# Power tables of a state-space layer made once for all groups, and dealt out at pace 0.85

## The chip, the cores and the metric

One core of a Trainium2 chip. The metric is the device time of one execution in microseconds (us). Two times are compared: the kernel before and the kernel after the change, with the same inputs and outputs.

## What is computed

A backbone of two layers on 512 latent tokens and 256 context tokens of width 1024. Layer 0 is attention, layer 1 a bidirectional diagonal state-space layer (S5); each layer has a SwiGLU feed-forward part before and after its mixer, with RMS norms and modulation around every part. The S5 mixer has 64 groups of 16 channels, each with 64 complex states in each of two directions:

```python
dt = exp(log_step); a = exp(lam_re * dt) * (cos(lam_im * dt) + 1j * sin(lam_im * dt))
f  = (a - 1) / lam ;  bb = f * b
x[t] = a * x[t-1] + bb @ u[t] ;  y[t] = real(c @ x[t]) + d * u[t]     # forward and backward
```

The kernel does the recurrence in blocks of 8 tokens. For that it needs, for each group and state, the powers a^0 to a^8, and for 96 blocks the phases of u^k, where u is the unit part of a^8. They depend on the weights alone and can be made long before the layer.

## The kernel before

**Feed-forward parts.** Nearly all time goes to matmuls of 128x128 weight tiles with 512 latent and 256 context columns. To keep precision each f32 weight tile is split into a high part (`whi`, ScalarE, L760) and a low part (`wlo`, mostly VectorE, L770), and each product is three matmuls (`mm3`, L869 to L871). A part runs in four chunks of 6, 5, 5 and 6 hidden tiles. In a chunk each hidden tile has two `w13` rows (8 k steps each), then VectorE multiplies gate and up (`w13_out`, L1067), ScalarE writes the high part `gh` (L918) and VectorE the low part `gl` (L921); the `w2` rows of the chunk follow and need all its hidden tiles, the last one last.

**Crossings.** From one part to the next a planned order (`cross`, L2608) runs the last rows, the norm sums (POOL among others), the new norm and the first rows of the next part. While it runs, background work is held (`hush`).

**Background work.** `s5_task` (L1948) is a Python generator that makes the S5 tables. It is put on the list `bg` in the crossing from attention to the second feed-forward part, and `rate` is set to `S5RATE` there (L2668). When the program is written, every stretch of PE work calls `tick` (L813) with its charged time (columns / 2400 per matmul); unless held, `pump` (L700) adds charge x `rate` to a credit of at most 8.0 and runs the generator to its next `yield` as long as the credit is above 0. The number a yield gives is taken off the credit. So pace and yields decide where the instructions stand in each engine's queue; each engine works its queue in order. Whatever is left when `need("s5")` is called in the crossing to the S5 layer (L2676) is issued there in one piece.

**The tables.** An opening (L1966 to L2058, all on VectorE but two sines) makes a (`A1`), the factor `F` and the unit phases (`un`) for all 64 groups; its yields sum to 28.2. Then `table(m)` (L2071) runs eight times, for 8 groups each:
- `bb` from `s5bc` and `F` (L2078 to L2084, VectorE);
- `pm`, the powers 0 to 8, by three complex products (`pmul`, `cmul`), and `ua`, the phase and its six squarings (`sq`), of tiles with 8 groups (L2087 to L2107, VectorE); `cmul` is six instructions (L1954 to L1959);
- `s5pw`, the powers in two orders, by eight copies (L2111 to L2114, VectorE);
- four times for two groups each: `s5v` by six products (L2133 to L2135), copies into `s5Bd` (L2137 to L2141), all VectorE; six POOL instructions (L2175 to L2179); `wout`, transposes on PE (L2186); `kout`, eight small matmuls on PE (L2148) that need `s5v` and `s5Bd`; `kcopy` (L2155 to L2164);
- the phase table `s5T` by doublings on POOL from `ua` (L2206 to L2225).

The results go to DRAM by 20 stores a table on SP's queue (L2121), and the S5 layer loads them per 8 groups (L2267 to L2281). The yields of a table sum to 92.3: 1.5 for `bb`, 0.6 + 3 x 1.0 + 6 x 1.0 for `pm` and `ua`, 1.2 for `s5pw`, 49.9 for the four quarters, 3.5, and 26.6 for the phase table. In a quarter, 1.5 follow the `s5Bd` copies, 4.5 the POOL instructions, 1.5 more, then comes `kout`. Between the crossings' ends the two feed-forward parts charge 419.8 and 435.2 us of PE time.

Of the kernel before, what the change touches and what calls it, by code (L numbers as in the profile page):

```python
# [10 lines left out]
F32 = mybir.dt.float32  # L11
# [5 lines left out]
P = 128  # L17
# [10 lines left out]


SC = (-1.5, -1.5, -1.3, -0.8, -0.25)  # L30
S5RATE = 1.0
PAIR = 1
LPS = (2,)
CP = [3.0, 3.0, 1.0, 1.3]
# [377 lines left out]
class Model:  # L412
# [837 lines left out]
    def attn(self, a, parts):  # L1250
# [153 lines left out]
        def split_nodes(n, hi, lo, deps, prio, acq=(), alloc=None, pool=False):  # L1404

            def fh():
                if alloc:
                    alloc()
                o, i = hi()
                nc.scalar.activation(o, i, AF.Copy)  # L1410

            def fl():
                o, i = lo()
                (nc.gpsimd if pool else nc.vector).tensor_tensor(o, i, hi()[0].bitcast(F32), op=ALU.subtract)
            h = G.add(ACT, cost[ACT](n), fh, deps, prio, acq)
            l = G.add(POOL if pool else DVE, cost[POOL if pool else DVE](n), fl, [h], prio)
            return h, l
# [49 lines left out]
        def spread(box):  # L1467
            box["h"], box["l"] = [st["A"].tile([P, 512], F32R, tag="pt" + x, name=f"pt{x}{self.uid()}", bufs=4)
                                  for x in ("h", "l")]

        def turned(blocks, deps, prio):

            box = {}
            n = len(blocks) * P

            def ft():
                box["t"] = self.sbank()
                for i, (b, c) in enumerate(blocks):
                    nc.tensor.transpose(box["t"][:, i * P:(i + 1) * P], b["p"][:, c:c + P], self.ident)
            T = G.add(PE, 0.11 * len(blocks), ft, deps, prio, ("st",))  # L1480
            h, l = split_nodes(n, lambda: (box["h"][:, :n], box["t"][:, :n]), lambda: (box["l"][:, :n], box["t"][:, :n]),
                               [T], prio, ("pt",), alloc=lambda: spread(box))
            T.free["st"].append(l)
            return box, n, T, h, l

# [21 lines left out]
        def weighted(hd, keys, vt, deps):  # L1507
# [4 lines left out]
            for j, (kt, blocks, cols, dn) in enumerate(keys):  # L1512
                prio = hd + (j + 0.5) / 7
                tb, n, T, h, l = turned(blocks, dn, prio)
                reads.append(T)

# [431 lines left out]
    def s5_task(self):  # L1948
        nc, io = self.nc, self.io
        v = nc.vector  # L1950

        def cmul(eng, outr, outi, ar, ai, br, bi, t):

            eng.tensor_tensor(t[0], ar, br, op=ALU.mult)  # L1954
            eng.tensor_tensor(t[1], ai, bi, op=ALU.mult)
            eng.tensor_tensor(outr, t[0], t[1], op=ALU.subtract)
            eng.tensor_tensor(t[0], ar, bi, op=ALU.mult)
            eng.tensor_tensor(t[1], ai, br, op=ALU.mult)
            eng.tensor_tensor(outi, t[0], t[1], op=ALU.add)  # L1959

        def gen():
            self.s5_open()
            sb, pp = self.sb, self.pp
            G = 64
            new = lambda name, shape, dt=F32, pool=sb: pool.tile(shape, dt, name=name)
            dsk = new("s5d", [16, G])  # L1966
            nc.sync.dma_start(out=dsk, in_=io["s5d"])
            A1 = new("s5A1", [P, 2, G])
            un = new("s5un", [P, 2, G])
# [4 lines left out]
            for tag, k in (("s5t0", 4), ("s5t1", 4), ("s5t3", 1)):  # L1974
                w = sb.tile([P, k, G], F32, tag=tag, name="s5w_" + tag)
# [30 lines left out]
            n, r = t[0], t[1]  # L2006
# [40 lines left out]
            sq = lambda o, i, q: cmul(v, o[0], o[1], i[0], i[1], i[0], i[1], q)  # L2047
# [8 lines left out]
            v.tensor_copy(un[:, 0], u2[0])  # L2056
            v.tensor_copy(un[:, 1], u2[1])
            yield 2.0  # L2058
            NG = 2
            Bd = new("s5Bd", [P, 2, NG, 64])  # L2060
            nc.gpsimd.memset(Bd, 0.0)
# [9 lines left out]
            def table(m):  # L2071
                gs = slice(m * 8, m * 8 + 8)
# [10 lines left out]
                v.tensor_tensor(bb[:, 1], q[:, 0], q[:, 1], op=ALU.add)  # L2083
                v.tensor_scalar(ci, ci, -1.0, None, op0=ALU.mult)  # L2084
                yield 1.5

                pm = sb.tile([P, 2, 9, 8], F32, tag="s5pm", name=f"s5pm{m}")  # L2087
                ua = sb.tile([P, 2, 7, 8], F32, tag="s5ua", name=f"s5ua{m}")
                sc = sb.tile([P, 2, 4, 8], F32, tag="s5sc", name=f"s5sc{m}")
                v.memset(pm[:, 0, 0], 1.0)  # L2090
                v.memset(pm[:, 1, 0], 0.0)
                for c in (0, 1):
                    v.tensor_copy(pm[:, c, 1], A1[:, c, gs])
                    v.tensor_copy(ua[:, c, 0], un[:, c, gs])

                def pmul(lo, n):
                    s_, o_ = slice(1, n + 1), slice(lo + 1, lo + n + 1)
                    b0, b1 = (pm[:, c, lo:lo + 1].to_broadcast([P, n, 8]) for c in (0, 1))
                    cmul(v, pm[:, 0, o_], pm[:, 1, o_], pm[:, 0, s_], pm[:, 1, s_], b0, b1,
                         [sc[:, 0, 0:n], sc[:, 1, 0:n]])  # L2100
                yield 0.6
                for lo, n in ((1, 1), (2, 2), (4, 4)):
                    pmul(lo, n)
                    yield 1.0
                for k in range(6):
                    sq((ua[:, 0, k + 1], ua[:, 1, k + 1]), (ua[:, 0, k], ua[:, 1, k]), [sc[:, 0, 0], sc[:, 1, 0]])
                    yield 1.0  # L2107
                pw = sb.tile([P, 2, 2, 8, 8], F32, tag="s5pw", name=f"s5pw{m}")
                ge = lambda x: x.rearrange("p e g -> p g e")
                for c in (0, 1):  # L2110
                    v.tensor_copy(pw[0:64, 0, c], ge(pm[0:64, c, 7::-1]))  # L2111
                    v.tensor_copy(pw[64:128, 0, c], ge(pm[64:128, c, 0:8]))
                    v.tensor_copy(pw[0:64, 1, c], ge(pm[0:64, c, 8:0:-1]))
                    v.tensor_copy(pw[64:128, 1, c], ge(pm[64:128, c, 1:9]))  # L2114
                yield 1.2
                cost = 0.75
                later, stores = [], []

                def flush():
                    for o, x in stores:  # L2120
                        nc.sync.dma_start(out=o, in_=x)  # L2121
                    stores.clear()
                for hf in range(8 // NG):
                    hs = slice(hf * NG, hf * NG + NG)
                    S4 = [P, NG, 8, 16]

                    vk = [sb.tile([P, NG, 144], F32, tag=f"s5v{i}", name=f"s5v{m}{hf}{i}") for i in range(2)]
                    t2 = sb.tile(S4, F32, tag="s5v2", name=f"s5v2{m}{hf}")
# [14 lines left out]
                    def kout(vk=vk):  # L2143
                        ps = self.bank()
                        for g in range(NG):
                            o = ps[0:64, g * 144:(g + 1) * 144]
# [59 lines left out]
                n, ng = 96, 4  # L2206
                for g0 in range(0, 8, ng):
                    gg = slice(g0, g0 + ng)
                    T = [sb.tile([P, ng, n], F32, tag=f"s5t{i}", name=f"s5T{m}{g0}{i}") for i in (0, 1)]
                    R = [sb.tile([P, ng, 32], F32, tag=f"s5t{i}", name=f"s5R{m}{g0}{i}") for i in (2, 3)]  # L2210
                    g_.memset(T[0][:, :, 0:1], 1.0)
                    g_.memset(T[1][:, :, 0:1], 0.0)
                    k, lev = 1, 0
                    while k < n:
                        w = min(k, n - k)
                        ur, ui = (ua[:, c, lev, gg].unsqueeze(2).to_broadcast([P, ng, w]) for c in (0, 1))
                        cmul(g_, T[0][:, :, k:k + w], T[1][:, :, k:k + w], T[0][:, :, 0:w], T[1][:, :, 0:w], ur, ui,
                             [R[0][:, :, 0:w], R[1][:, :, 0:w]])
                        yield 0.8 + 0.015 * w * ng
                        flush()  # L2220
                        k, lev = k + w, lev + 1
                    for c in (0, 1):
                        stores.append((self.dr[m, :, c, gg], T[c]))
                    yield 2.0
                    flush()  # L2225
            for m in range(8):
                yield from table(m)
            self.bg_done.add("s5")
            yield 0.0
        return ("s5", gen())  # L2230


# [401 lines left out]
    def build(self):  # L2634
# [20 lines left out]
        def end_mods():  # L2655
# [12 lines left out]
        self.cross(attn, (0, 1), ffn01, (0, 2), a2, lambda: (self.yc.release(), self.bg.append(self.s5_task()),  # L2668
                                                           setattr(self, "rate", S5RATE)),
                   lambda: (attn.close(), self.ffn_pool()))  # L2670
# [223 lines left out]
```

## Time and profile before

| | us |
|---|---|
| three runs | 3020.44, 3026.11, 3029.89 (median 3026.11) |
| the profiled execution, its own time | 3023.44 |
| span of its profile | 3021.4 |
| mean granted TensorE clock | 0.97 |

The span is what the profiler saw from the first to the last instruction. Engines are PE (matmul), PEld (weight load beside it), DVE (VectorE), ACT (ScalarE), POOL (GpSimd) and SP (which issues transfers). Matmuls are pipelined: the length of one in a row of the timeline is longer than the distance to the next. A wait is put down to the work that released it last.

### The profile page before, as it was taken

Reading aid. Unit: us, or ns where it says so; the run is one execution under the profiler, and the core shown is the slowest. Engines: PE = TensorE matmul, PEld = TensorE weight load, DVE = VectorE, ACT = ScalarE, POOL = GpSimd, SP = SyncE. Lnnn points to the kernel's source line nnn. Section 1 sums busy time; section 2 is a strip of 40 time slices with the busy share of each in tenths; the row PEclk is TensorE's granted clock in tenths of the full one; section 3 lists DMA queues with packets and bytes.
Section 4 is the critical chain, followed back from the end, with each engine's and each line's share of the span. In section 5 each row is a group of like instructions: output and inputs, shape, how many; then the busy total and the mean of one; then the engine's idle time right before and its main releaser. Section 6 shows DMA issues by size and latency. Waiting matters only on the chain. (4 is left out here: it accounts for less than half of the span.)

```text
span 3021.4 us, 42503 instructions
## 1 busy us (share of the span) xinstructions
PE 2839.2 (94%) x16008; PEld 2453.4 (81%) x16008; DVE 1921.5 (64%) x3621; ACT 1084.0 (36%) x1897; POOL 902.7 (30%) x1281
## 2 busy tenths in 40 slices
PE   4999989989999989999999899999998899999997
PEld 3888778878778778888887788888887897988886
DVE  8798989675588577465465765456337695543344
ACT  3432232344587652222222432222124444432222
POOL 4122222252354351334434534434405100300001
PEclk9999999999799999999999999999999899999998
DMA  6365556633000222323232333232323463232332
GB/s 245 105 217 185 193 183 231 220 108 120 5 24 22 92 97 86 101 70 95 87 99 82 104 110 89 87 99 71 99 67 104 174 214 98 93 109 92 100 101 70
DMA packets 140813, 343.59 MB, mean 114 GB/s; under 512 B 13632, under 2 KB 61248, under 8 KB 138560
## 3 DMA queue, kind: packets, MB, share of 16 engines
q1 hardware_dynamic: 140608, 340.88, 35.0%
q8 instruction: 126, 2.06, 0.3%
q14 instruction: 79, 0.65, 0.1%
HBM read 311.53 MB, written 29.29 MB: 113 GB/s over the span
## 5 line engine op out<-in xcount | busy, mean ns | idle before, releaser
L869 PE MATMUL mm<-ahi,whi 128*128 128x512 f32 (+1 forms) x2128 | 740.2, 348 | 21.8 <-ACT ahi L555 17.6
L870 PE MATMUL mm<-alo,whi 128*128 128x512 f32 (+1 forms) x2128 | 736.0, 346 | 10.5 <-DVE alo L556 7.6
L871 PE MATMUL mm<-ahi,wlo 128*128 128x512 f32 (+1 forms) x2128 | 728.3, 342 | 4.3 <-DVE wlo L770 4.3
L770 DVE TENSOR_TENSOR wlo<-raw,whi 128x1024 fp32r<-128x1024 f32 (+2 forms) x391 | 464.0, 1189 | 354.0 <-ACT whi L760 336.0
L760 ACT ACTIVATE whi<-raw 128x1024 fp32r<-128x1024 f32 (+2 forms) x411 | 392.8, 956 | 289.1 <-PE mm L870 141.2
L869 PEld LDWEIGHTS mm<-ahi,whi 128*128 128x128 f32 x2128 | 406.5, 191 | 81.2 <-ACT ahi L555 19.4
L870 PEld LDWEIGHTS mm<-alo,whi 128*128 128x128 f32 x2128 | 406.3, 191 | 62.0 <-DVE alo L556 10.8
L871 PEld LDWEIGHTS mm<-ahi,wlo 128*128 128x128 f32 x2128 | 405.1, 190 | 56.1 <-DVE wlo L770 5.5
L869 PE MATMUL mm<-gh,whi 128*128 128x512 f32 x992 | 351.8, 355 | 20.1 <-ACT gh L918 20.1
L870 PE MATMUL mm<-gl,whi 128*128 128x512 f32 x992 | 350.6, 353 | 1.2 <-DVE gl L921 1.2
L871 PE MATMUL mm<-gh,wlo 128*128 128x512 f32 x992 | 347.4, 350 | 1.6 <-DVE wlo L770 1.6
L651 DVE SCALAR_TENSOR_TENSOR mj<-mw,cb 128x1024 bf16<-128x1024 f32 x182 | 258.2, 1419 | 23.4 <-DMA mw<-in_mod_wT_dram 20.4
L918 ACT ACTIVATE gh<-tmp 128x512 fp32r<-128x512 f32 (+1 forms) x135 | 73.7, 546 | 539.9 <-DVE tmp L1067 539.1
L907 POOL TENSOR_TENSOR S<-S,tmp 128x512 f32<-128x512 f32 (+1 forms) x25 | 27.5, 1101 | 689.3 <-ACT tmp L906 688.8
L869 PEld LDWEIGHTS mm<-gh,whi 128*128 128x128 f32 x992 | 188.7, 190 | 50.5 <-ACT gh L918 21.9
L667 POOL TENSOR_TENSOR mw<-mw,cb 128x1024 f32<-128x1024 f32 x42 | 116.9, 2784 | 376.9 <-DVE mj L651 312.4
L870 PEld LDWEIGHTS mm<-gl,whi 128*128 128x128 f32 x992 | 188.5, 190 | 27.7 <-DVE gl L921 3.2
L871 PEld LDWEIGHTS mm<-gh,wlo 128*128 128x128 f32 x992 | 188.0, 190 | 28.2 <-DVE wlo L770 2.0
L2175 POOL TENSOR_TENSOR s5t<-s5pw,s5bb 128x256 f32<-128x256 f32 x128 | 92.8, 752 | 391.5 <-PE mm L2186 257.8
L1067 DVE TENSOR_TENSOR tmp<-tmp,mm 128x512 f32<-128x512 f32 (+1 forms) x135 | 77.4, 574 | 177.3 <-PE mm L871 171.9
L279 POOL TENSOR_TENSOR S<-S,tmp 128x256 f32<-128x256 f32 (+3 forms) x116 | 134.5, 1162 | 136.1 <-ACT tmp L276 129.4
L921 DVE TENSOR_TENSOR gl<-tmp,gh 128x512 fp32r<-128x512 f32 (+1 forms) x135 | 94.8, 702 | 82.9 <-ACT gh L918 82.9
(463 smaller groups left out, 5230.6 us busy)
## 6 DMA issues: line engine op xcount, KB each, us to landing
raw<-in_w_dram SPq DMA_DIRECT2D x210, 512.0 KB, 3.7
mw<-in_mod_wT_dram SPq DMA_DIRECT2D x128, 512.0 KB, 4.2
raw<-in_w_dram SPq DMA_DIRECT2D x88, 384.0 KB, 3.1
raw<-in_w_dram SPq DMA_DIRECT2D x64, 320.0 KB, 3.0
raw<-in_w_in_dram SPq DMA_DIRECT2D x23, 512.0 KB, 3.6
m0d<-in_mod_wT_dram SPq DMA_DIRECT2D x16, 512.0 KB, 8.0
raw<-in_w_out_dram SPq DMA_DIRECT2D x16, 512.0 KB, 3.2
s5v<-s5v SPq DMA_DIRECT2D x64, 128.0 KB, 2.7
```

The costliest lines, as they stand in the source:

```text
L279: add = lambda e: lambda: e.tensor_tensor(S(), S(), q["t"][:, :n], op=ALU.add)
L651: self.nc.vector.scalar_tensor_tensor(junk, w, 1.0, self.cb[v], op0=ALU.mult, op1=ALU.mult, accum_out=self.modc[l][:, v, t:t + 1])
L667: nc.gpsimd.tensor_tensor(w, w, self.cb[v], op=ALU.mult)
L760: self.nc.scalar.activation(hi[:, :n], raw[:, :n], AF.Copy)
L770: (eng or self.nc.vector).tensor_tensor(lo[:, :n], raw[:, :n], hi[:, :n].bitcast(F32), op=ALU.subtract)
L869: mm(out, whi, xhi, start=first, stop=False)
L870: mm(out, whi, xlo, start=False, stop=False)
L871: mm(out, wlo, xhi, start=False, stop=last)
L918: nc.scalar.activation(hi, src, AF.Copy)
L921: nc.vector.tensor_tensor(lo, src, hi.bitcast(F32), op=ALU.subtract)
L1067: nc.vector.tensor_tensor(t[:, :n], t[:, :n], bk[g][:, cs], op=ALU.mult)
L2175: g_.tensor_tensor(o, x, y, op=ALU.mult)
```

## The change

`S5RATE` goes from 1.0 to 0.85. The powers `pm` and the squared phases `ua` are made once, after the opening, in tiles for all 64 groups, and `table(m)` reads its slice of them. The yields change with it: the `s5pw` copies are charged 2.2 instead of 1.2, the yields of `pm` and `ua` (0.6, three and six times 1.0) leave the table, and the new shared part yields 1.2, 1.5, 1.8, 2.4 and six times 1.5. The scratch tiles share the tags `s5t0` and `s5t1`.

```diff
-S5RATE = 1.0
+S5RATE = 0.85
...
             yield 2.0
+
+            pm = new("s5pm", [P, 2, 9, G])
+            ua = new("s5ua", [P, 2, 7, G])
+            sc = [sb.tile([P, 4, G], F32, tag=f"s5t{i}", name=f"s5sc{i}") for i in (0, 1)]
+            v.memset(pm[:, 0, 0], 1.0)
+            v.memset(pm[:, 1, 0], 0.0)
+            for c in (0, 1):
+                v.tensor_copy(pm[:, c, 1], A1[:, c])
+                v.tensor_copy(ua[:, c, 0], un[:, c])
+            yield 1.2
+            for lo, n in ((1, 1), (2, 2), (4, 4)):
+                s_, o_ = slice(1, n + 1), slice(lo + 1, lo + n + 1)
+                b0, b1 = (pm[:, c, lo:lo + 1].to_broadcast([P, n, G]) for c in (0, 1))
+                cmul(v, pm[:, 0, o_], pm[:, 1, o_], pm[:, 0, s_], pm[:, 1, s_], b0, b1, [x[:, 0:n] for x in sc])
+                yield 1.2 + 0.3 * n
+            for k in range(6):
+                sq((ua[:, 0, k + 1], ua[:, 1, k + 1]), (ua[:, 0, k], ua[:, 1, k]), [x[:, 0] for x in sc])
+                yield 1.5
...
                 yield 1.5
-
-                pm = sb.tile([P, 2, 9, 8], F32, tag="s5pm", name=f"s5pm{m}")
-                ua = sb.tile([P, 2, 7, 8], F32, tag="s5ua", name=f"s5ua{m}")
-                sc = sb.tile([P, 2, 4, 8], F32, tag="s5sc", name=f"s5sc{m}")
-                ...
-                    v.tensor_copy(pm[:, c, 1], A1[:, c, gs])
-                    v.tensor_copy(ua[:, c, 0], un[:, c, gs])
-                ...
-                yield 0.6
-                for lo, n in ((1, 1), (2, 2), (4, 4)):
-                    pmul(lo, n)
-                    yield 1.0
-                for k in range(6):
-                    sq(...)
-                    yield 1.0
...
-                    v.tensor_copy(pw[0:64, 0, c], ge(pm[0:64, c, 7::-1]))
+                    v.tensor_copy(pw[0:64, 0, c], ge(pm[0:64, c, 7::-1, gs]))
...
-                yield 1.2
+                yield 2.2
...
+                    g1 = slice(m * 8 + g0, m * 8 + g0 + ng)
...
-                        ur, ui = (ua[:, c, lev, gg].unsqueeze(2).to_broadcast([P, ng, w]) for c in (0, 1))
+                        ur, ui = (ua[:, c, lev, g1].unsqueeze(2).to_broadcast([P, ng, w]) for c in (0, 1))
```

## Rows read from the trace of the kernel before

**Rows 1.** The profile's page, part 1: busy time of each engine with its share of the span and its number of instructions.

```profile
PE 2839.2 (94%) x16008; PEld 2453.4 (81%) x16008; DVE 1921.5 (64%) x3621; ACT 1084.0 (36%) x1897; POOL 902.7 (30%) x1281
```

**Rows 2.** Windows over five stretches (us from the span's start), all engines: length, busy time with instructions of PE, PEld, DVE, ACT and POOL, then the granted clock as a share of full speed, the DMA share and GB/s.

```profile
1184.00:1654.00 470.00, 454.96 (x2562) 392.92 (x2561) 267.88 (x831) 104.47 (x175) 185.14 (x454) 0.98 0.29 87
1654.00:1767.00 113.00, 102.40 (x612) 90.11 (x611) 84.95 (x132) 51.60 (x85) 53.81 (x40) 0.97 0.32 102
1767.00:2171.00 404.00, 401.93 (x2328) 349.41 (x2327) 212.67 (x612) 93.41 (x157) 175.37 (x437) 1.00 0.30 92
2171.00:2271.00 100.00, 100.00 (x524) 85.69 (x523) 31.21 (x39) 25.00 (x38) 3.81 (x5) 1.00 0.24 74
2271.00:2355.00 84.00, 70.06 (x417) 61.42 (x415) 62.67 (x92) 37.28 (x62) 43.55 (x33) 0.94 0.36 113
```

**Rows 3.** The waits of PE between 1100 and 2300 us, longest in total first: us in total, times, longest.

```profile
PE mm L2148 <- DVE s5Bd L2141: 10.5, 5, 5.5
PE mm L869 <- ACT gh L918: 6.6, 1, 6.6
```

**Rows 4.** The timeline of PE, at the six waits: start and length in us, engine, line, operation, out<-in, shape, count, and in brackets the idle time before it and what released it.

```profile
1208.68 2.15 PE L2148 MATMUL mm<-s5v,s5Bd 128*64 128x144 f32 x8 [5.52 <-DVE s5Bd L2141]
...
1320.09 1.44 PE L2148 MATMUL mm<-s5v,s5Bd 128*64 128x144 f32 x8 [2.05 <-DVE s5Bd L2141]
...
1538.18 1.35 PE L2148 MATMUL mm<-s5v,s5Bd 128*64 128x144 f32 x8 [0.83 <-DVE s5Bd L2141]
...
1647.57 0.79 PE L869 MATMUL mm<-gh,whi 128*128 128x512 f32 x1 [6.64 <-ACT gh L918]
...
1975.04 1.35 PE L2148 MATMUL mm<-s5v,s5Bd 128*64 128x144 f32 x8 [1.19 <-DVE s5Bd L2141]
...
2083.93 1.25 PE L2148 MATMUL mm<-s5v,s5Bd 128*64 128x144 f32 x8 [0.88 <-DVE s5Bd L2141]
```

**Rows 5.** The timeline of DVE from 1634 to 1647 us, columns as in rows 4: table 4's squarings, its `s5pw` copies and `s5v` products, and behind them L1067 of the feed-forward layer.

```profile
1634.08 0.16 DVE L1954 TENSOR_TENSOR s5sc<-s5ua 128x8 f32<-128x8 f32 x1
...
1638.78 0.96 DVE L770 TENSOR_TENSOR wlo<-raw,whi 128x768 fp32r<-128x768 f32 x1
1639.65 0.20 DVE L2111 COPY s5pw<-s5pm 64x64 f32<-64x64 f32 x1
...
1640.35 0.55 DVE L2114 COPY s5pw<-s5pm 64x64 f32<-64x64 f32 x1
...
1642.23 0.75 DVE L2133 TENSOR_TENSOR s5v<-s5pw,s5bc 128x256 f32<-128x256 f32 x1
...
1646.17 0.68 DVE L1067 TENSOR_TENSOR tmp<-tmp,mm 128x512 f32<-128x512 f32 x1
```

**Rows 6.** Windows behind three of the waits, columns as in rows 2.

```profile
1209.00:1212.00 3.00, 3.00 (x11) 2.37 (x10) 1.64 (x5) 0.35 (x1) 0.00 (x0) 0.50 0.49 115
1321.00:1325.00 4.00, 4.00 (x16) 3.18 (x15) 1.62 (x6) 0.35 (x1) 0.00 (x0) 0.57 0.41 141
1647.60:1652.40 4.80, 4.80 (x11) 3.49 (x12) 3.28 (x10) 2.01 (x3) 0.00 (x0) 0.51 0.24 44
```

**Rows 7.** The timeline of DVE from 1184 to 1192 us, columns as in rows 4: the last product of the opening (64 columns), `bb` of table 0 (128 columns), its copies and fills, power products and the first squaring.

```profile
1184.31 0.22 DVE L1954 TENSOR_TENSOR s5w_s5t<-s5un 128x64 f32<-128x64 f32 x1
...
1185.51 0.19 DVE L2056 COPY s5un<-s5w_s5t 128x64 f32<-128x64 f32 x1
...
1185.73 0.28 DVE L2078 TENSOR_TENSOR s5q<-s5bc,s5F 128x128 f32<-128x128 f32 x1
...
1187.31 0.22 DVE L2084 TENSOR_SCALAR s5bc<-s5bc 128x128 f32<-128x128 f32 x1
1187.48 0.16 DVE L2093 COPY s5pm<-s5A 128x8 f32<-128x8 f32 x1
...
1187.77 0.16 DVE L1954 TENSOR_TENSOR s5sc<-s5pm 128x8 f32<-128x8 f32 x1
...
1188.72 0.18 DVE L1954 TENSOR_TENSOR s5sc<-s5pm 128x16 f32<-128x16 f32 x1
...
1190.77 0.18 DVE L1954 TENSOR_TENSOR s5sc<-s5pm 128x32 f32<-128x32 f32 x1
...
1191.87 0.17 DVE L1954 TENSOR_TENSOR s5sc<-s5ua 128x8 f32<-128x8 f32 x1
```

**Rows 8.** The timeline of all engines from 1780 to 1784 us, columns as in rows 4: a product of 256 columns on DVE (three instructions) without POOL beside them, and the start of two k steps of a row on PE.

```profile
1780.37 0.42 DVE L2133 TENSOR_TENSOR s5v<-s5pw,s5bc 128x256 f32<-128x256 f32 x1
...
1781.50 0.17 DVE L2137 COPY s5v<-s5bc 128x32 f32<-128x32 f32 x1
...
1782.62 0.40 PE L869 MATMUL mm<-ahi,whi 128*128 128x512 f32 x1
...
1783.67 0.40 PE L869 MATMUL mm<-ahi,whi 128*128 128x512 f32 x1
```

**Rows 9.** The waits of DVE between 1080 and 2300 us, columns as in rows 3.

```profile
DVE s5ua L2094 <- POOL s5R L1958: 8.3, 4, 3.1
```

**Rows 10.** The instructions that touch `s5T` and the DRAM table `s5r`: line, engine, operation, count, ns least/median/most, first and last start in us, shapes. The last line is the loads of the table in the layer.

```profile
L1959 POOL TENSOR_TENSOR s5T<-s5R,s5R x112: 208/254/1322, 1265.8 to 2171.8; 128x128 f32<-128x128 f32 x32, 128x4 f32<-128x4 f32 x16, 128x8 f32<-128x8 f32 x16, 128x16 f32<-128x16 f32 x16
...
L2273 SPq DMA_DIRECT2D s5r<-s5r x8: 319/360/704, 2351.4 to 2486.1; - x8
```

**Rows 11.** The timeline of POOL from 1156 to 1203 us, columns as in rows 4.

```profile
1201.13 0.66 POOL L2175 TENSOR_TENSOR s5t<-s5pw,s5bb 128x256 f32<-128x256 f32 x1 [42.71 <-DVE s5pw L2112]
```

More of the change, by code (lines that the diff above doesn't have):

```diff
@@ L2085, in table @@
                 yield 1.5
-                pm = sb.tile([P, 2, 9, 8], F32, tag="s5pm", name=f"s5pm{m}")
-                ua = sb.tile([P, 2, 7, 8], F32, tag="s5ua", name=f"s5ua{m}")
-                sc = sb.tile([P, 2, 4, 8], F32, tag="s5sc", name=f"s5sc{m}")
-                v.memset(pm[:, 0, 0], 1.0)
-                v.memset(pm[:, 1, 0], 0.0)
-                for c in (0, 1):
-                    v.tensor_copy(pm[:, c, 1], A1[:, c, gs])
-                    v.tensor_copy(ua[:, c, 0], un[:, c, gs])
[L2096 to L2100, printed above, removed]
-                yield 0.6
-                for lo, n in ((1, 1), (2, 2), (4, 4)):
-                    pmul(lo, n)
-                    yield 1.0
-                for k in range(6):
-                    sq((ua[:, 0, k + 1], ua[:, 1, k + 1]), (ua[:, 0, k], ua[:, 1, k]), [sc[:, 0, 0], sc[:, 1, 0]])
-                    yield 1.0
                 pw = sb.tile([P, 2, 2, 8, 8], F32, tag="s5pw", name=f"s5pw{m}")
@@ L2110, in table @@
                 for c in (0, 1):
-                    v.tensor_copy(pw[0:64, 0, c], ge(pm[0:64, c, 7::-1]))
-                    v.tensor_copy(pw[64:128, 0, c], ge(pm[64:128, c, 0:8]))
-                    v.tensor_copy(pw[0:64, 1, c], ge(pm[0:64, c, 8:0:-1]))
-                    v.tensor_copy(pw[64:128, 1, c], ge(pm[64:128, c, 1:9]))
-                yield 1.2
+                    v.tensor_copy(pw[0:64, 0, c], ge(pm[0:64, c, 7::-1, gs]))
+                    v.tensor_copy(pw[64:128, 0, c], ge(pm[64:128, c, 0:8, gs]))
+                    v.tensor_copy(pw[0:64, 1, c], ge(pm[0:64, c, 8:0:-1, gs]))
+                    v.tensor_copy(pw[64:128, 1, c], ge(pm[64:128, c, 1:9, gs]))
+                yield 2.2
                 cost = 0.75
```

## The prediction

> **What bounds the kernel now.** The profile's first row: TensorE (PE) is busy 94% of a span of 3021.4 us, VectorE (DVE) 64%, GpSimd (POOL) 30% [rows 1]. Only the stretch in which the tables of the state-space layer are made beside two feed-forward layers can change, so I read it by windows next [rows 2]: 1184 to 1654 us and 1767 to 2171 us carry table work, 2171 to 2271 carries none. PE is the bound in all three, DVE is half busy. What can be won is therefore only what PE waits there. The waits of PE between 1100 and 2300 us [rows 3] have two large entries: 10.5 us in 5 waits of L2148 (the table's own small matmul, `kout`) for L2141 on DVE, and one wait of 6.6 us of L869 for `gh` of L918.
>
> The timeline gives these six waits their places [rows 4]. The five of L2148 are all the first `kout` of a table (tables 0, 1, 3, 6, 7), none a later one. So something that stands only at a table's start makes DVE late. The sixth, at 1647.57, has the same cause one step further: on DVE, table 4's squarings run from 1634.08 to 1638.78, its `s5pw` copies and `s5v` products until 1646.17, and only then comes L1067, the product from which ACT makes the `gh` that PE waits for [rows 5]. All six are one queue: DVE works off the table's opening burst in order, and PE's work stands behind it.
>
> Behind three of the waits the granted clock is at its lower level (1.2 GHz) while PE works again: 0.50 for 3.0 us, 0.57 for 4.0 us, 0.51 for 4.8 us [rows 6]. At half speed such a stretch costs the missing share: 1.5 + 1.7 + 2.35 = 5.6 us.
>
> **The parts of the change.** *Removed from each table:* two fills, four copies, three power products and six squarings, 60 instructions on DVE. Start to start: copies and fills 1187.48 to 1187.77, the first product 0.95, the third 1.10 [rows 7], so about 3.05 for three, five squarings 4.7 [rows 5], so 5.6 for six; 0.3 + 3.05 + 5.6 = 9.0 us a table, 72 us in eight. *Added once:* the same 60 on 64 groups. A complex product of 64 columns takes 1.2 us (1184.31 to 1185.51), of 128 columns about 1.6 (1185.73 to 1187.31) [rows 7], of 256 columns 2.3 (twice 1780.37 to 1781.50) [rows 8]; 1.2 + 1.6 + 2.3 + six times 1.2, and 0.6 for copies, is 12.9 us. DVE is relieved of 59 us, which alone is worth nothing, because it is not the bound: only the waits count. A wait goes too: L2094 waited four times, 8.3 us in all, for POOL to finish with the old `s5ua` [rows 9]; with one tile that is never rewritten it cannot. POOL's and PE's instructions stay the same, the 20 stores a table puts on SP's queue too.
>
> *The pace.* Background work is dealt out by PE time charged in the program: a w13 row of 768 columns is charged 0.96 us per k and takes 1.05 (1782.62 to 1783.67 [rows 8]), so one charged us is 1.094 real ones. Before, the task's yields sum to 28.2 for the opening and 92.3 a table, 766.6 in all. After, a table loses 9.6 and gains 1.0 (the copies are now charged 2.2), 83.7, and the shared part adds 15.9: 28.2 + 15.9 + 669.6 = 713.7.
>
> *Table start, before.* From L2078 (1185.73) to the last `s5Bd` copy DVE needs 1.75 + 9.0 + 2.6 for its products, powers and `s5pw` copies [rows 5, 7], and 3.2 to 4.9 for `s5v` and `s5Bd` (the larger when POOL works beside it: L2133 takes 0.42 alone [rows 8], 0.75 beside it [rows 5]): 16.6 to 18.3 us. Its share of the ordinary layer is 31% (31.21 of 100 us without table work [rows 2]). This is charged 15.6, or 17.1 real us, of which the layer takes 5.3: DVE falls behind by 5 to 6.5 us. Between the last copy and `kout` 7.5 are charged, 8.2 us of room at most. The 256-column steps and whatever DVE was behind already use up the rest; that five of eight tables miss it by 0.8 to 5.5 us [rows 4] fits.
>
> *Table start, after.* 7.6 to 9.3 us on DVE, charged 7.0, at pace 0.85 9.0 real us, less 2.8 for the layer: it falls behind by 1.4 to 3.1, and the room grows to 7.5/0.85 x 1.094 = 9.65. If all `s5pw` copies took as long as the slowest form does now (0.57 [rows 5]; they now read with a wider stride), that is 2 us more, still inside. So the four waits of tables 1 to 7 go (4.95 us).
>
> *Table 0.* At its first `kout` DVE is now 8.2 + 5.5 = 13.7 us behind, about 7 of them brought along. The slower pace stretches the opening by 3.9 us, of which DVE gains 2.7; the shared powers need 12.9 + 6.4 in 15.9/0.85 x 1.094 = 20.5 us and win another 1.2; so it comes about 3 us late to table 0, 4.5 to 6 at the copies, inside 9.65. The 5.5 us go. But table 0 now starts 42.5 charged us into the layer, and the first `gh` matmuls follow at 46.1: the last `gh` is needed five k steps (5.25 us) after, its own chain takes 2, and DVE is 3 to 5 us behind: a new wait of 0 to 2 us. I take 2, the bad end, as the 6.6 us wait of the same kind is the nearest row.
>
> *The wait at 1647.* The crossing to the next layer starts 419.8 charged us in. Before, that is the start of table 4; after, 8 in hand + 0.85 x 419.8 = 364.9, and table 3 has then 69.7 of its 83.7: in POOL's phase table, with nothing on DVE. The 6.6 us go, unless POOL's lag hits the crossing's own sums there.
>
> *The end.* 855.0 charged us lie between the two crossings' ends; 855.0 x 0.85 + 8 = 734.8 against 713.7 leaves 21.1 credits, 27 real us at this pace before the crossing at about 2271. Now the last POOL product is at 2171.8; the end moves to about 2244, and the next layer reads its first table at 2351.4 [rows 10]. The cover is there: 2171 to 2271 holds no table work, with POOL at 4% [rows 2]. In it the weight loads now find table 7's stores ahead of them in SP's queue, as they do before in the other stretches, where no load is among PE's large waits [rows 3].
>
> **The sum.** 10.5 + 6.6 + 5.6 = 22.7 us, less 2: about 20.7. The profiled execution took 3023.4 us, 2.7 under the median of 3026.1: 3002.7 there, 3005 against the median.
>
> A rule that speaks against the change: the Trainium skill, "GPSIMD Engine Reference", section Specifications, has POOL share its way to SBUF with two-input DVE instructions. The trace agrees, by the 0.42 and 0.75 above. [...]
>
> **Rivals.** *The first table stays late.* Wide powers slowed as L2133 was would take 12.9 x 0.75/0.42 = 23 us; with DVE 10 us more behind, PE would wait some 10 to 12 us in all at the first `gh` and table 0's `kout`, with 2 us of half clock after it. 22.7 - 13 leaves about 10 us, 3015 to 3018. By the same rule of the Trainium skill this is what happens if POOL is busy then. Against it: POOL's first table product starts only at 1201.1, released by the `s5pw` copies [rows 11]. What could make DVE late anyway is that the 7 us brought along are inferred. Chance 0.17. *The waits move.* The crossings, about 112 and 84 us long, are not PE-bound (102.40 of 113, 70.06 of 84 [rows 2]); POOL's phase work now stands ahead of the first and table 7 ahead of the second, and what PE gains it waits there: 3020 to 3030. Chance 0.11. *Slower: the pace is too low.* If the task is not through when the second crossing begins, its rest is issued in one piece where the pool is given back. The point is 713.7 - 8 over 855.0, a pace of 0.825. A phase table, 26.6 charged, would then stand alone before the state-space layer: 3005 + 27, and the wait for its store and load, up to 3040. For it: 0.85 is only 3% above that point. Against it: yields and charges are counted, not measured. Chance 0.06.
>
> **How the numbers follow.** The forecast has 0.66. Its own range is 2999 to 3012: all 22.7 and a lucky run below, the 6.6 us wait kept above. Taking in the first rival to 3020 and the spread of the runs (3020 to 3030), the range is 2997 to 3021. A measurement of this kernel can tell about 0.3%, 9 us, from no change: faster holds the forecast and half of the first rival, 0.73; same the other half and most of the second, 0.20; slower 0.07.
>
> **What the profile would show.** Right: no L2148 wait on L2141 in PE's waits, no wait near 1640 us on `gh`, no half clock between 1200 and 1330; the last POOL product near 2230 to 2245; `s5ua` made once by about 60 instructions. Wrong: a wait at the first `kout` or the first `gh` matmul (DVE's lag mis-sized), longer crossings (waits moved), or table work behind the second crossing's start (pace).

## The result, and the profile after

The changed kernel took 2994.97 us (median of 4 runs, 2992.80 to 3001.87) against 3024.45 us of the kernel before (4 runs, 3020.44 to 3029.89): a ratio of 0.9911, interval 0.9892 to 0.9931. In a later comparison it gave 2997.36 against 3021.85: 0.9927, interval 0.9910 to 0.9943. The profiled execution took 3001.87 us with a span of 2999.9, against 3023.44 and 3021.4: 21.6 us less; the forecast for the profiled execution was 3002.7. Executions of either kernel differ by about 10 us for a reason that the change doesn't touch (last section), so the traces, not the medians, tell what it is worth.

The page's first row, which answers to [rows 1]:

```profile
PE 2838.6 (95%) x16008; PEld 2456.4 (82%) x16008; DVE 1852.1 (62%) x3201; ACT 1084.4 (36%) x1897; POOL 898.4 (30%) x1281
```

DVE has 420 instructions less, as counted (480 removed, 60 added), and 69.4 us less busy time, where I had 59 from start to start. PE's busy time over the whole span is the same to 0.6 us, but other stages are in that figure. Between the two matmuls that bound the stretch measured below, PE's idle time fell from 41.7 to 22.3 us and its busy time from 1170.4 to 1166.9. Where the idle time went, say the windows that answer to [rows 2] (columns as there):

```profile
1184.00:1654.00 470.00, 470.00 (x2657) 406.69 (x2656) 229.53 (x585) 112.92 (x187) 170.24 (x409) 1.00 0.30 90
1654.00:1767.00 113.00, 104.23 (x627) 93.94 (x626) 76.20 (x113) 48.49 (x80) 54.15 (x67) 0.92 0.35 107
1767.00:2171.00 404.00, 404.00 (x2339) 351.69 (x2338) 191.36 (x461) 93.20 (x158) 153.77 (x365) 1.00 0.29 88
2171.00:2271.00 100.00, 100.00 (x519) 85.41 (x517) 41.01 (x58) 29.84 (x44) 42.63 (x101) 1.00 0.32 98
```

In the first and the third PE is busy without a gap at a granted clock of 1.00; before, they held 15.0 and 2.1 us of idle time, the first at 0.98. The windows stand at fixed times, and all work has moved forward in them: the second now begins inside the crossing. The fourth, empty of table work before, holds table 7's end (POOL 42.63 us instead of 3.81).

The waits of PE from 1140 to 2400 us, the three largest in total:

```profile
PE mm L245 <- DVE tmp L1171: 5.6, 2, 2.8
PE st L891 <- POOL r L304: 3.7, 5, 1.0
PE mm L2337 <- DVE u L2329: 3.1, 1, 3.1
```

The first two stood in the kernel before as 5.6 and 4.2, both in the crossings. The entries of [rows 3] are gone: `kout`, now L2144, and L869 for `gh` of L918 wait nowhere. The three windows of half clock behind them [rows 6] went along. The first crossing gave 1.5 us back: PE runs there at a granted clock of 0.80 for 20 us (1690 to 1710), where the same work had 0.91 before (1710 to 1730).

Table 0 on DVE (timeline, columns as in rows 4), answering to [rows 7]: first fill of the powers, the first product of each width, the first and last squaring, `bb`, and the last copy before `kout`:

```profile
1188.07 0.11 DVE L2063 MEMSET s5pm<- 128x64 f32 x1
...
1189.65 0.22 DVE L1954 TENSOR_TENSOR s5sc<-s5pm 128x64 f32<-128x64 f32 x1
...
1190.95 0.29 DVE L1954 TENSOR_TENSOR s5sc<-s5pm 128x128 f32<-128x128 f32 x1
...
1195.78 0.42 DVE L1954 TENSOR_TENSOR s5sc<-s5pm 128x256 f32<-128x256 f32 x1
...
1199.03 0.22 DVE L1954 TENSOR_TENSOR s5sc<-s5ua 128x64 f32<-128x64 f32 x1
...
1207.36 0.23 DVE L1959 TENSOR_TENSOR s5ua<-s5sc,s5sc 128x64 f32<-128x64 f32 x1
1207.51 0.28 DVE L2096 TENSOR_TENSOR s5q<-s5bc,s5F 128x128 f32<-128x128 f32 x1
...
1220.61 0.18 DVE L2137 COPY s5Bd<-s5bb 64x32 f32<-64x32 f32 x1
```

From start to start the wide products took 1.30 (64 columns), 1.60 (128) and 2.38 us (256), the six squarings 1.2 to 1.3 each, all shared work 13.3 where 12.9 was forecast. `kout` follows on PE with no idle time in brackets before it, 2.2 us after that copy ended:

```profile
1222.98 1.20 PE L2144 MATMUL mm<-s5v,s5Bd 128*64 128x144 f32 x8
```

The end of the table work, answering to [rows 10]:

```profile
L1959 POOL TENSOR_TENSOR s5T<-s5R,s5R x112: 208/254/1371, 1288.1 to 2226.0; 128x128 f32<-128x128 f32 x32, 128x4 f32<-128x4 f32 x16, 128x8 f32<-128x8 f32 x16, 128x16 f32<-128x16 f32 x16
...
L2270 SPq DMA_DIRECT2D s5r<-s5r x8: 319/368/638, 2331.0 to 2466.3; - x8
```

The last product starts at 2226.0 instead of 2171.8, and the table's first load in the layer at 2331.0 instead of 2351.4. The profiled execution of after came 2.0 us later than that of before to the start of the feed-forward layer that carries tables 0 to 3, which has nothing to do with the tables; from there to the first load it gained 22.4 us.

That stretch, from the start of that layer to the end of the crossing ahead of the state-space layer, is the measure for the experiments: in each trace I took the time between the same two matmuls of PE's order. The last column is the median against that of the kernel before in the same comparison.

| kernel | stretch, us against before | median, us |
|---|---|---|
| the change | -23.0 | -29.5 |
| the change again | -22.9 | -24.5 |
| powers once, pace 1.0 | -14.2 | -12.2 |
| powers once, pace 0.90 | -17.3 | -19.8 |
| powers once, pace 0.80 | -0.3 | +1.6 |
| powers eight times, pace 0.95 | -9.1 | -8.4 |
| powers eight times, pace 0.90 | -22.8 | -22.7 |
| powers eight times, pace 0.87 | -2.9 | -3.6 |
| powers eight times, pace 1.0, later `kout` | -3.0 | -6.3 |
| the change, POOL kept busy | -12.0 | -10.4 |

### The profile page after: what moved, and what is told of

The parts are those of the page before. It is cut to its first block, busy times and chain, and to the rows that moved or that the text cites. A ratio compares the mean times of both kernels' runs of the same rounds, so it can differ in the third digit from the quotient of the medians.

```text
span 2999.9 us, 42053 instructions
## 1 busy us (share of the span) xinstructions
PE 2838.6 (95%) x16008; PEld 2456.4 (82%) x16008; DVE 1852.1 (62%) x3201; ACT 1084.4 (36%) x1897; POOL 898.4 (30%) x1281
## 5 line engine op out<-in xcount | busy, mean ns | idle before, releaser
L869 PE MATMUL mm<-ahi,whi 128*128 128x512 f32 (+1 forms) x2128 | 740.0, 348 | 20.9 <-ACT ahi L555 16.7
L770 DVE TENSOR_TENSOR wlo<-raw,whi 128x1024 fp32r<-128x1024 f32 (+2 forms) x391 | 461.4, 1182 | 376.0 <-ACT whi L760 360.4
L760 ACT ACTIVATE whi<-raw 128x1024 fp32r<-128x1024 f32 (+2 forms) x411 | 392.8, 956 | 296.8 <-PE mm L870 161.7
L869 PEld LDWEIGHTS mm<-ahi,whi 128*128 128x128 f32 x2128 | 406.7, 191 | 80.2 <-ACT ahi L555 18.8
L869 PE MATMUL mm<-gh,whi 128*128 128x512 f32 x992 | 350.8, 354 | 13.5 <-ACT gh L918 13.5
L651 DVE SCALAR_TENSOR_TENSOR mj<-mw,cb 128x1024 bf16<-128x1024 f32 x182 | 262.6, 1443 | 24.5 <-DMA mw<-in_mod_wT_dram 21.8
L918 ACT ACTIVATE gh<-tmp 128x512 fp32r<-128x512 f32 (+1 forms) x135 | 73.7, 546 | 491.8 <-DVE tmp L1067 490.7
L869 PEld LDWEIGHTS mm<-gh,whi 128*128 128x128 f32 x992 | 188.4, 190 | 43.3 <-ACT gh L918 14.9
L1067 DVE TENSOR_TENSOR tmp<-tmp,mm 128x512 f32<-128x512 f32 (+1 forms) x135 | 77.5, 574 | 186.3 <-PE mm L871 186.3
L279 POOL TENSOR_TENSOR S<-S,tmp 128x256 f32<-128x256 f32 (+3 forms) x116 | 134.5, 1162 | 135.4 <-ACT tmp L276 128.7
L1064 ACT ACTIVATE tmp<-mm 128x512 f32<-128x512 f32 (+1 forms) x135 | 63.0, 506 | 274.1 <-PE mm L871 274.1
```

Of the source, the lines that this page charges most:

```text
L279: add = lambda e: lambda: e.tensor_tensor(S(), S(), q["t"][:, :n], op=ALU.add)
L651: self.nc.vector.scalar_tensor_tensor(junk, w, 1.0, self.cb[v], op0=ALU.mult, op1=ALU.mult, accum_out=self.modc[l][:, v, t:t + 1])
L760: self.nc.scalar.activation(hi[:, :n], raw[:, :n], AF.Copy)
L770: (eng or self.nc.vector).tensor_tensor(lo[:, :n], raw[:, :n], hi[:, :n].bitcast(F32), op=ALU.subtract)
L869: mm(out, whi, xhi, start=first, stop=False)
L918: nc.scalar.activation(hi, src, AF.Copy)
```

## The experiments

**Powers once, the old pace.** The changed kernel with one constant set back.

```diff
-S5RATE = 0.85
+S5RATE = 1.0
```

> Powers made once, as after the change, but pace 1.0. Theory A (the gain is the six waits behind the opening burst of a table; either less work in the burst or more room after it takes them away): no wait at the first kout of tables 1 to 7 and none at 1647 us, because 7.6 to 9.3 us of VectorE work are charged 7.0 with 8.2 us of room behind; table 0 stays late, since 7 us are brought along and the wide powers win nothing at pace 1.0: 2 to 6 us of waiting at its kout or at the first gh matmul. Sum 13 to 20 us faster than before. Rival B (the slower pace makes the gain): waits like those of before at most tables, at most 6 us faster.

3009.62 us, ratio 0.9958 (0.9941 to 0.9975). PE's waits from 1140 to 2400 us, the entries that concern the tables:

```profile
PE mm L2144 <- DVE s5Bd L2137: 2.6, 1, 2.6
...
PE mm L869 <- ACT gh L918: 0.8, 1, 0.8
```

The first stands at table 0. The second is what is left of the 6.6 us at the crossing, at the same matmul (timeline of PE):

```profile
1639.63 0.51 PE L869 MATMUL mm<-gh,whi 128*128 128x512 f32 x1 [0.85 <-ACT gh L918]
```

So the four waits of tables 1 to 7 and most of the one at the crossing are gone without any help of the pace; behind the wait at table 0 PE runs at a granted clock of 0.57 for 8 us (the window from 1214 to 1222 us). Half of the edit brings 14 of 23 us.

**The change once more**, to see what of the 21.6 us repeats.

> The changed kernel once more, for its time beside the three others on one chip. From the waits in the profiles: 20 to 23 us faster than before, ratio 0.992 to 0.9935; if the median of 27 us (0.9911) holds, 4 to 6 us come from somewhere that the waits of PE between 1100 and 2300 us do not show.

The profiled execution took 2993.4 us, 8.5 less than the first one of the same kernel, with 22.9 us in the stretch instead of 23.0. What repeats is the stretch.

**The old tables, a slower pace.** The kernel before with one constant changed: all eight-fold powers stay on DVE.

```diff
-S5RATE = 1.0
+S5RATE = 0.9
```

> Powers made eight times, as before, pace 0.9 (at 0.85 the task does not end before the second crossing). Theory A: burst 3.5 to 5.2 us behind instead of 4.8 to 6.5, room 9.1 instead of 8.2 us: no wait at the first kout of tables 1 to 7; the crossing falls into the phase table of table 3, so the wait of 6.6 us goes too; 1 to 3 us stay at table 0. Sum 16 to 20 us faster, although VectorE does all its 72 us of powers. Rival C (the 59 us of VectorE work that the change saves are the gain): at most 5 us faster.

2999.17 us, ratio 0.9922 (0.9904 to 0.9941), and 22.8 us in the stretch: all of the change's gain, with none of its relief of DVE. The largest waits of PE from 1140 to 2400 us are the crossings' own:

```profile
PE mm L245 <- DVE tmp L1171: 5.6, 2, 2.8
PE st L891 <- POOL r L304: 3.7, 5, 1.0
PE mm L2340 <- DVE u L2332: 3.1, 1, 3.1
```

So either half suffices for the later tables, the pace alone also for table 0 and for the rest at the crossing, and the halves don't add up: 14 and 23 make 23. That the gain is DVE's 59 us is out.

**More room ahead of `kout`, nothing else.** The kernel before; 5 charged us are moved from the phase table's 14 yields to the one between the burst's last copy and `kout`.

```diff
-                    yield 1.5
+                    yield 1.5 + (5.0 if hf == 0 else 0.0)
                     ps = kout()
...
-                        yield 0.8 + 0.015 * w * ng
+                        yield 0.8 + 0.015 * w * ng - 5.0 / 14
```

> Powers made eight times and pace 1.0, as before; only 5.0 more are charged between the s5Bd copies and the first kout of each table, and 5.0 less in its phase table, so that a table's sum stays 92.3. Theory A: VectorE's queue is as late as before, but PE comes to kout 5.5 us later: the five waits at kout (10.5 us, and 3.2 us of half clock) go or shrink below 1 us in all, the wait of 6.6 us at the crossing stays: 10 to 14 us faster. Rival C: no change, within 3 us.

A miss: 3015.56 us, ratio 0.9988 (0.9975 to 1.0001), 3.0 us in the stretch. PE's waits from 1140 to 1660 us:

```profile
PE mm L869 <- ACT gh L918: 8.5, 1, 8.5
PE mm L871 <- DVE wlo L770: 5.1, 4, 2.1
PE mm L2148 <- DVE s5Bd L2141: 2.0, 2, 1.7
```

The `kout` waits fell from 10.5 to 2.0 us, as meant, but the `gh` wait at the crossing grew from 6.6 to 8.5, and a wait came up that the kernel before did not have, for instance here (timeline of PE, in brackets the idle time):

```profile
1521.82 0.50 PE L871 MATMUL mm<-gh,wlo 128*128 128x512 f32 x1 [1.69 <-DVE wlo L770]
...
1528.47 0.50 PE L871 MATMUL mm<-ahi,wlo 128*128 128x512 f32 x1 [1.12 <-DVE wlo L770]
...
1627.18 0.58 PE L871 MATMUL mm<-gh,wlo 128*128 128x512 f32 x1 [2.08 <-DVE wlo L770]
```

The weights' low parts (`wlo`) stand in DVE's queue behind the same burst. Where PE meets the burst first can be moved; DVE is as late as before, and the next thing that PE wants of it is late instead. Table 0 shows it: PE still starts `kout` at 1208.65, where it did at 1208.68 (1201.25 in this trace, which runs 7.4 us ahead there), but now after an idle time of 0.3 instead of 5.5 us, with other work done in between.

**The old tables at 0.95 and 0.87.** Two more paces, one short of what table 0 needs, one below what the task needs to end in time.

```diff
-S5RATE = 1.0
+S5RATE = 0.95
```
```diff
-S5RATE = 1.0
+S5RATE = 0.87
```

> Powers made eight times, pace 0.95, between 1.0 (six waits) and 0.9 (none was left). If VectorE's lag at a table's start sets the gain: about 1 us less lag and 0.4 us more room than at 1.0, so the wait at table 0 falls from 5.5 to about 3.5 us, table 1 keeps about 1 us, the others none; the last w13 row before the crossing now falls into the phase table of table 3, so the wait of 6.6 us goes. 12 to 18 us faster than before. If the pace acts in another way than by these waits: in proportion, 10 to 12 us, with the 6.6 us kept.

> Powers made eight times, pace 0.87: 855.0 x 0.87 + 8 = 751.9 of 766.6 charged fit before the second crossing, so 14.7 (the second half of the last phase table) are issued in one piece in the crossing. The rival 'pace too low': about 14 us of POOL work in one piece there delay the S5 layer by 5 to 15 us, and 8 to 18 us of the gain of pace 0.9 (23 us by the trace) stay. If the load of the last table and the pool's memory have time enough: as fast as pace 0.9.

At 0.95: 3013.06 us, ratio 0.9970 (0.9957 to 0.9982), less than expected. PE's waits from 1140 to 2400 us:

```profile
PE st L296 <- POOL S L279: 3.7, 1, 3.7
...
PE mm L2148 <- DVE s5Bd L2141: 2.5, 1, 2.5
PE mm L869 <- ACT gh L918: 1.6, 1, 1.6
```

Of the 17 us of `kout` and `gh` waits 2.5 are left at table 0, and 1.6 came up at 2113.70, in the second feed-forward layer. The first crossing became 7.9 us longer: table 4's opening burst is on DVE until 1656.6, among the layer's last rows (L1108), and PE waits for a norm sum (L279) that is late; the run at 0.90 below shows what it was late for. That is the prediction's rival "the waits move", at a pace that the change doesn't use and by another way than POOL's work.

At 0.87 the sum of "the end" gives 855.0 x 0.87 + 8 = 751.9 of 766.6 charged us, so 14.7 are issued in one piece in the second crossing. 3017.85 us, ratio 0.9996 (0.9984 to 1.0007): 21.7 us won up to that crossing, 18.8 lost in it. The wait of PE:

```profile
2352.85 1.23 PE L891 MATMUL st<-ident,r 128*128 128x128 f32 x4 [19.99 <-POOL r L304]
```

and POOL's timeline ahead of it:

```profile
2335.74 0.10 POOL L2211 MEMSET s5T<- 128x4 f32 x1 [3.99 <-DMA s5r<-s5T]
...
2349.33 0.45 POOL L1959 TENSOR_TENSOR s5T<-s5R,s5R 128x128 f32<-128x128 f32 x1
2352.03 0.11 POOL L2245 MEMSET rho<- 128x8 f32 x1 [2.24 <-DMA s5r<-s5T]
2352.09 0.70 POOL L304 TENSOR_TENSOR r<-r,mhalf 128x2 f32<-128x2 f32 x1
```

The norm's `r` is POOL work too and stands behind the rest of the phase table, which twice waits for its own stores.

**The change at 0.80 and 0.90.**

```diff
-S5RATE = 0.85
+S5RATE = 0.80
```
```diff
-S5RATE = 0.85
+S5RATE = 0.90
```

> Powers made once, pace 0.80: 692.0 of 713.7 charged fit, 21.7 (most of the last phase table, some 23 us of POOL work) are issued in one piece in the second crossing. The rival 'pace too low': 10 to 25 us slower than the change, so about as fast as before. Otherwise as fast as the change.

> Powers made once, pace 0.90: between the change (0.85, no wait left) and 1.0 (3.6 us of waits at table 0). If only VectorE's lag counts: at pace 0.85 VectorE was done 2.2 us before the first kout of table 0; 0.9 takes 0.55 us of room and adds 1 to 2 us of lag, so 0 to 1 us of waiting there, none elsewhere, and within 2 us of the change. What it wins is distance to the second crossing: 777.5 charged against 713.7, 63.8 left instead of 21.1.

At 0.80, 21.7 charged us are left over (713.7 - 692.0): 3023.02 us, ratio 0.9996 (0.9979 to 1.0013); 23.4 us won up to the second crossing, 23.1 lost in it, at the same place as above:

```profile
PE st L891 <- POOL r L304: 26.9, 6, 23.8
```

At 0.90: 3000.37 us, ratio 0.9944 (0.9928 to 0.9959), and a miss by a few us: no wait at `kout` or `gh`, but the first crossing is 6 us longer, with this wait in it (timeline of PE):

```profile
1659.67 1.86 PE L296 MATMUL st<-ones,S 128*128 128x1 f32 x8 [4.01 <-POOL S L279]
```

There table 3 is through and table 4's opening burst stands on DVE just as the crossing begins; at 0.85 the crossing begins within table 3's phase table, with nothing of the tables on DVE, and this wait is absent. The row names POOL, but POOL was idle before its sum; it waited for ACT (timelines of DVE, ACT and POOL):

```profile
1653.03 0.68 DVE L1195 TENSOR_TENSOR y<-mm,y 128x512 f32<-128x512 f32 x1
...
1656.18 1.06 ACT L760 ACTIVATE whi<-raw 128x1024 fp32r<-128x1024 f32 x1 [3.98 <-DMA raw<-in_w_dram]
1657.15 0.61 ACT L276 ACTIVATE tmp<-y 128x512 f32<-128x512 f32 x1
...
1657.90 1.72 POOL L279 TENSOR_TENSOR S<-S,tmp 128x512 f32<-128x512 f32 x1 [3.63 <-ACT tmp L276]
```

The row that is to be summed was there at 1653.7, but its step on ACT (L276) stands in ACT's queue behind the split of a weight tile (L760), and that tile's load had not landed. In the change the same step starts at 1661.22, 0.1 us after its row. The 0.95 run has the same chain (L760 waits 3.07 us for its load, then L276, then L279). Such a load is issued when `wlo` (L770) has read the old tile: between 1600 and 1680 us SP's queue waits 43.6 us for that, so lateness on DVE passes to the loads. Table 3's last phase stores stand among them in the same queue and wait 9.7 us for POOL's `s5T`, while at 0.85 the first store of that phase table is issued at 1751.97, behind the crossing. Which of the two began it is not shown.

**The change with POOL kept busy during the wide products.** Added: 36 needless POOL products of 256 columns on a tile of their own, four after each wide product and squaring.

```diff
+            ja, jb = (sb.tile([P, 256], F32, tag=f"s5t{i}", name=f"s5j{i}") for i in (2, 3))
+            nc.gpsimd.memset(ja, 1.0)
+
+            def busy(n):
+                for _ in range(n):
+                    nc.gpsimd.tensor_tensor(jb, ja, ja, op=ALU.mult)
...
+                busy(4)
                 yield 1.2 + 0.3 * n
...
+                busy(4)
                 yield 1.5
```

> The changed kernel with 36 needless products of 128x256 on POOL (about 0.65 us each) issued among the wide powers, 4 behind each; nothing reads them. Contention theory (the first rival of the prediction): the wide products take up to 1.8 times as long, VectorE comes 6 to 10 us later to table 0, PE waits 4 to 10 us at the first gh matmul or the first kout. Otherwise: the products are as long as before, no new wait, the time of the change.

3011.04 us, ratio 0.9963 (0.9949 to 0.9978): 11 us of the stretch's gain gone. POOL did not wait for DVE: it ran its products at once, 1183.81 to 1211.76 us (timeline of POOL):

```profile
1183.81 27.95 POOL L2070 TENSOR_TENSOR s5j<-s5j 128x256 f32<-128x256 f32 x36
```

so they stood beside the opening's end and the power products, and were over before the squarings. DVE beside and behind them (timeline):

```profile
1198.30 0.63 DVE L1954 TENSOR_TENSOR s5sc<-s5pm 128x64 f32<-128x64 f32 x1
1198.85 0.21 DVE L1955 TENSOR_TENSOR s5sc<-s5pm 128x64 f32<-128x64 f32 x1
1199.10 0.52 DVE L1956 TENSOR_TENSOR s5pm<-s5sc,s5sc 128x64 f32<-128x64 f32 x1
...
1201.04 0.72 DVE L1954 TENSOR_TENSOR s5sc<-s5pm 128x128 f32<-128x128 f32 x1
...
1207.45 0.83 DVE L1954 TENSOR_TENSOR s5sc<-s5pm 128x256 f32<-128x256 f32 x1
...
1212.84 0.21 DVE L1954 TENSOR_TENSOR s5sc<-s5ua 128x64 f32<-128x64 f32 x1
```

Up to three times the time of the same instruction in the change (0.22, 0.29, 0.42), and the first squaring starts 13.8 us later than there, 12.4 without the executions' own offset of 1.4 (the same matmuls ahead of the tables). Of these 12.4 us 6.4 arose in the opening's end, 6.0 in the fills, copies and wide products. PE meets it in two places (timeline of PE):

```profile
1212.97 0.80 PE L871 MATMUL mm<-gh,wlo 128*128 128x512 f32 x1 [2.77 <-DVE wlo L770]
...
1224.42 0.50 PE L869 MATMUL mm<-gh,whi 128*128 128x512 f32 x1 [3.69 <-ACT gh L918]
```

6.5 us of waits, and a granted clock of 0.57 in the 7 us behind the first (3.0 us) and of 0.86 in the 12 us about the second (1.7 us): 11.2 together. So the first rival's mechanism is real. Its price came near (10 us more on DVE and 13 lost, against 12.4 and 11), but in part by luck: half of the lag arose in the opening, which the rival left out, and the squarings, 7.2 of its 12.9 us, had no POOL beside them. The change escapes it because POOL has nothing to do there: its first table product starts at 1212.97, after 52.5 us of idle time.

## Why the prediction was right, point by point

**The bound and the sum.** Right. The sum had 10.5 + 6.6 + 5.6 = 22.7 us to win, less 2; the stretch gave 23.0 and 22.9. All six waits and the half clock behind them went, and the two executions of the change, 8.5 us apart in time, differ by 0.1 us inside the stretch: all the rest lies outside it. That 22.7 and 23.0 lie so close is partly luck: the idle time fell by 19.4 us, 2.3 more than the six waits, and the busy time by 3.5, 2.1 less than the half clock, because the first crossing ran at a lower clock than before.

**"Table 0": the term that was mis-sized.** I took 2 us for a new wait at the first `gh`, from the nearest row, the 6.6 us wait. There is none: the last `gh` of the chunk is there 2.9 us before PE reads it (timelines of ACT and PE in the change),

```profile
1209.94 0.63 ACT L918 ACTIVATE gh<-tmp 128x512 fp32r<-128x512 f32 x1 [8.35 <-DVE tmp L1067]
...
1213.44 0.40 PE L869 MATMUL mm<-gh,whi 128*128 128x512 f32 x1
```

and DVE is through 2.2 us ahead of `kout`. At pace 1.0 table 0 waits 2.6 us at `kout` and not at `gh`, so it is the pace that clears `kout`; the `gh` matmul above waits only with POOL kept busy (3.7 us), so the place was one that can wait, but not in this kernel.

**"The parts of the change".** 12.9 us forecast for the shared powers, 13.3 measured. `s5ua`'s wait for POOL [rows 9] is gone. The parts were rightly costed, but which of them brings the gain was only half seen: the old tables at 0.90 bring all of it. What the removed work does is to make a slow pace affordable, and at 0.90 the old tables could afford it already: no run here shows time won by the shared powers beyond what that pace wins alone, and at 0.90 they won less (17.3 against 22.8 us), for what stood at the first crossing. With the old tables the pace must stay above (766.6 - 8)/855.0 = 0.887, and 0.87 proved too low; with the new ones above 0.825. At 0.85 the change ends with 21.1 charged us in hand, the old tables at 0.90 with 10.9.

**"Table start": the room.** Here I counted two things, how far DVE falls behind and how much room lies ahead of `kout`. The room alone was worth 3 us where I expected 10 to 14. What counts is DVE's lag: PE reads `wlo` and `gh` from the same queue, and `kout` was only the first to feel it. The working also counts 1.5 charged us twice, once in the burst (15.6, and 7.0 after) and once in the 7.5 of room. With 14.1 and 5.5, DVE falls behind by 6.0 to 7.7 us before and 2.7 to 4.4 after. That is still inside the room, and it fits the 2.2 us left at table 0 better: the working's 4.5 to 6 us of lag in 9.65 would have left 3.6 or more.

**"The wait at 1647".** It went, with table 3's phase table on POOL at the crossing, as worked out. The reserve named there was that POOL's lag may hit the crossing's own sums. At 0.90 and 0.95 they were late, and the crossing 6 and 7.9 us longer, but through ACT's queue and a weight load, with POOL idle.

**"The end".** Forecast 2244 us for the last POOL product, measured 2226.0: I had left out that everything before it moves forward by the gain itself, some 20 us. With it the count of yields and charges holds to a few us.

**The rivals.** "The first table stays late" did not happen, and a busy POOL was shown to bring such waits. "The waits move" did not happen at 0.85, but for the 1.5 us of lower clock in the first crossing. "Too low a pace" did not happen, and its point is bracketed: 14.7 charged us too many cost 18.8 us, 21.7 cost 23.1. Its place was right and its price of the right order (27 was for a whole phase table of 26.6 charged us), but not its sum: it was added to a time of 3005 that the runs undercut, so such kernels ended level with the one before, not slower. (The chances hold a small slip: the forecast's 0.66 and half of 0.17 are 0.745, not 0.73.)

**The median.** 2995 and 2997 instead of 3005, at the low edge of the range of 2997 to 3021, the first 2 us below it. Some 2 us of that are the wait that didn't come, and the kernel before was itself 1.7 us under the 3026.1 that the forecast counts from. In the two comparisons the medians fell by 29.5 and 24.5 us, the stretch by 23: the remainder is, by what the profiled executions show, how the executions on either side came out in a stage without tables (last section).

**Open.** What first made the weight loads late in the first crossing at 0.90 and 0.95. DVE's busy time fell by 10 us more than the powers' start-to-start times: the `s5v` tiles' instructions, 256 in both kernels, were busy 91.1 instead of 100.6 us, and the 128 copies into `s5Bd` 27.2 instead of 32.4. That they met POOL less often would explain it, but is not shown.

## What to carry to other kernels

Background work that is dealt out in bursts on an in-order engine makes its foreground late by the burst, and the bound engine waits wherever it first reads from that queue; moving that place moved the wait here, and a smaller burst or a slower deal removed it. The slowest pace is a sum that can be made beforehand (work charged over time charged), and cutting the work buys pace; a rest that doesn't fit cost about its own length in both runs that had one, at the place where it is issued in one piece. And where a burst meets a stage boundary matters too: the change at 0.85 and at 0.90, 5.7 us apart in the stretch, differs by what stands at the first crossing. Lastly, the engine that a wait's row names may itself have been waiting: at 0.90 the row named POOL, and three steps further back stood a weight load.

## What the runs showed of the hardware that was not expected

**DVE beside a busy POOL pays by the instruction, not by the column.** A 64-column product went from 0.22 to 0.52 or more, one of 128 from 0.29 to 0.72 at most, one of 256 from 0.42 to 0.83, one of 1024 (`wlo`) from 1.22 to 1.63: 0.3 to 0.45 us each. I had carried the factor of a 256-column product over to all widths; the short ones suffer three-fold. One in three of the 64- and 128-column products was untouched (0.21 at 1198.85), so was one `gl` of 512 columns (0.69 in both), and so was a product with one operand in PSUM (L1067, 512 columns, 0.68 and 0.67). I had also put the factor at 1.8 (0.75 over 0.42); the most that was seen is 3 (0.66 over 0.22). The Trainium skill, "GPSIMD Engine Reference", section Specifications, says that POOL's SBUF interfaces are shared with VectorE, with contention for DVE instructions that have two SBUF inputs; this run agrees for most of them, and shows the price. Why some products with two SBUF inputs escape, no run here shows.

**The granted clock differs between executions in a stage that is the same program.** Windows over 60 us of the attention part, well ahead of the tables, of the kernel before, the change and the change again (columns as in rows 2):

```profile
760.00:820.00 60.00, 56.50 (x249) 45.92 (x248) 33.00 (x89) 31.75 (x91) 19.49 (x18) 0.69 0.00 1
```
```profile
760.00:820.00 60.00, 55.67 (x239) 45.10 (x240) 31.78 (x88) 30.57 (x87) 19.50 (x18) 0.69 0.00 1
```
```profile
760.00:820.00 60.00, 53.71 (x294) 42.60 (x293) 40.16 (x111) 36.75 (x104) 23.92 (x24) 0.91 0.01 2
```

The third has more instructions done in the same 60 us at 0.91 instead of 0.69, and its execution took 2993.4 us against 3001.9 of the second. Of the eleven executions traced, eight show 0.69 in this window and three 0.89 to 0.91; these three come to the feed-forward layer of tables 0 to 3 between 6.6 and 7.4 us before the kernel before does, the eight between 0.2 us before and 3.7 us after. As far as these traces tell, this is most of the spread of 10 us between runs of one kernel; what decides it, no run here shows. A change that is worth 20 us in another stage is best measured between two fixed matmuls of the trace.
